# Interleaving saved up-projection products with the making of x1's blocks in a float32 hybrid decoder layer

## The chip, the core and the metric

The kernel runs on one core of a Trainium2 chip. The metric is the device time of one execution in microseconds (us). Before the change it was 2717.78 us, the median of 3 runs (2716.36 to 2719.78).

## What is computed

One post-norm decoder layer over x of shape (1, 512, 2048), all in float32:

```
m  = W_out( sum_n sigmoid(g_n(x)) * P_n(branch_n(x)) )      n in {DSA, S5, MoBA}
x1 = LayerNorm(alpha * x + m)        # gain ln1_g, bias ln1_b
h  = conv3(x1 @ w_up)                # 2048 -> 2 * 5632, causal, three taps, along the tokens
a, val = split(h, 2)
out = LayerNorm(alpha * x1 + (gelu(a) * val) @ w_down)      # gain ln2_g, bias ln2_b
```

The part that matters here is from the last quarter of `merged @ W_out` over the first LayerNorm and x1's transposition into the up projection, and then the down projection, which needs x1 once more as the residual. Float32 products are made of three float32r products: each operand is split into a high part `h` (a rounded copy, on ScalarE) and a low part `l` (the difference, on VectorE), and `h*h + h*l + l*h` are added in PSUM.

## The kernel before

Tokens are tiled into 4 tiles `t` of 128. The output projection runs in 4 chunks `c` of 512 columns; in the last chunk the second half of the contraction (8 of 16 blocks) is held in SBUF as split weights, and tile after tile is finished with it, so that a tile's residual, statistics and norm (`norm_tile`, lines 916 to 919) start while PE works on the next tile. `norm` (876 to 882) does the whole LayerNorm on VectorE in two passes: `(y - mu) * g1b` and `y * r + b1b`, with gain and bias broadcast to all partitions (`g1b`, `b1b`, line 884), and stores the finished x1 to DRAM (`resd`, from ScalarE's DMA queue) for the down projection.

The up projection multiplies in Strassen's manner, with two halves of the contraction, two halves (a, value) of the columns and two halves of the tokens: per pair `j` of 128-column blocks (`up_pair`, 1048 to 1093) seven products (`prod`, 1010) of 24 matmuls of 256 columns, named for the x1 operand that they read: `a11`, `q1`, `s2`, `a12`, `s3`, `a22`, `q4`. VectorE forms the weight sums `t1` to `t4` (`wsum`, 1004) and splits every weight operand (`hl`, 995). The x1 operands are blocks of 2 x 256 columns: `turn` (921) transposes x1 from `res` into a PSUM bank by four PE transposes, VectorE forms sums and differences of those banks, `block` (932) splits each. There are 28 blocks and 32 calls of `turn`. `a11` and `a12` need the first two token tiles alone, the rest need all four.

For the first six pairs (`NPRE = 6`) the products with `a11` and `a12` are done ahead (`ahead_of`, 1031) and saved to DRAM (`pred`); `up_pair` loads them as `p1` and `hf1` and does five products. In the program the ahead products stand after all blocks, as a loop of their own. The pool `upl`, which holds among others the second weight half (`raw2`), the sums (`ts`) and every third pair of split weights (`wh3`, `wl3`), is opened after `res` is released and lies over it.

The down projection (`down_mm`, 1156) runs 44 steps `f` for each half `u` of the columns: a step loads an activation block (`act_hl`) and a weight block (`w_hl`), splits both and multiplies for four token tiles. `LATE` (1190) names the steps at which x1's tiles (`y_`) and LayerNorm 2's vectors are loaded; `late` puts a copy of one column ahead so that the DMA is not issued earlier.

The order of the instructions on each engine is set by a scheduler that runs over the program with its own estimates and the priorities given (`tc.high_priority`); each engine then works strictly in that order and waits on semaphores.

Of the kernel before, what the change touches and what calls it, by code (L numbers as in the profile page):

```python
# [39 lines left out]
def tile_trunk(ctx: ExitStack, tc: tile.TileContext, x, rel_bias, w_in, cq_gain, ckv_gain,  # L40
# [791 lines left out]
    xq1 = ctx.enter_context(tc.tile_pool(name="xq1", bufs=16, reuse_waits="tile"))  # L832
    rx = ExitStack()
    rp = rx.enter_context(tc.tile_pool(name="rp", bufs=1, reuse_waits="tile"))
    res = rp.tile([P, NT, D], F32, name="res")
    lx = ExitStack()
# [11 lines left out]
    lp.tile([P, 40], F32, name="lpad")  # L848
# [4 lines left out]
    def bcast(pool, v, name):  # L853
        t_ = pool.tile([P, D], F32, name=name)
        nc.sync.dma_start(t_, bass.AP(tensor=v.tensor, offset=v.offset, ap=[[0, P], [1, D]]))
        return t_

# [26 lines left out]
    g1b, b1b = bcast(bcp, ln1_g[0], "g1b"), bcast(bcp, ln1_b[0], "b1b")  # L884
    mvs = {}
    for c in range(4):
        c0, n = 512 * c, 512
        xt = xr.tile([P, NT, n], F32, tag="xt", name="xt")
        nc.sync.dma_start(xt, x2[:, c0:c0 + n].rearrange("(t p) n -> p t n", p=P))
        banks = [mm_bank() for _ in range(NT)]  # L890
        for k0 in range(0, KD if c < 3 else KD // 2, 2):
            wh, wl = wunit(w_out[0], k0, 2, c0, n)
            for k in range(2):
                kk = k0 + k
                for t in range(NT):
                    tok_mm(banks[t], t, mT[kk][0], mT[kk][1], wh[:, k], wl[:, k], kk == 0, kk == KD - 1)
# [6 lines left out]
        ws = []  # L903
        for k0 in range(KD // 2, KD, 2):
            raw = load_raw(w_out[0], k0, 2, c0, n)
            for k in range(2):
                wh = xp.tile([P, 512], F32R, tag="x", name="lwh")
                wl = xp.tile([P, 512], F32R, tag="x", name="lwl")
                split_w(wh, wl, raw[:, k])
                ws.append((wh, wl))  # L910
        for t in range(NT):
            for kk in range(KD // 2, KD):
                tok_mm(banks[t], t, mT[kk][0], mT[kk][1], *ws[kk - KD // 2], False, kk == KD - 1)
# [17 lines left out]

    def block(name, kk, pool, src):
        h = pool.tile([P, 512], F32R, tag="x", name="x1h")
        l = pool.tile([P, 512], F32R, tag="x", name="x1l")
        split(h, l, src)
        for k in range(2):
            X[name, 2 * kk + k] = (h[:, 256 * k:256 * k + 256], l[:, 256 * k:256 * k + 256])

    with tc.high_priority(100):
        for t in range(2):  # L940
            norm_tile(t)
        for kk in range(4):
            block("a11", kk, xq1, turn(0, 0, kk))
        for kk in range(4):
            block("a12", kk, xq1, turn(0, 1, kk))
    for t in range(2, 4):
        norm_tile(t)
    lx.close()
    ux = ExitStack()
    right(ux, "upad").tile([P, 80], F32, name="upad")  # L950
    xq2 = right(ux, "xq2", 10)
    x21, s2 = [], []
    for kk in range(4):
        b21, b22, b11 = turn(2, 0, kk), turn(2, 1, kk), turn(0, 0, kk)
        x21.append(xq2.tile([P, 512], F32, tag="x", name="x21"))
        nc.scalar.activation(x21[kk], b21, AF.Copy)
        q1 = xq2.tile([P, 512], F32, tag="x", name="q1")
        nc.vector.tensor_sub(q1, x21[kk], b22)
        s2.append(xq2.tile([P, 512], F32, tag="x", name="s2"))
        nc.vector.tensor_sub(s2[kk], q1, b11)  # L960
        block("s2", kk, xp, s2[kk])
        block("q1", kk, xp, q1)
    for kk in range(4):
        s3 = xq2.tile([P, 512], F32, tag="x", name="s3")
        nc.vector.tensor_sub(s3, turn(0, 0, kk), x21[kk])
        block("s3", kk, xp, s3)
    for kk in range(4):
        block("a22", kk, xp, turn(2, 1, kk))
    for kk in range(4):
        nc.vector.tensor_add(s2[kk], s2[kk], turn(0, 1, kk))  # L970
        block("q4", kk, xq2, s2[kk])
    rx.close()


# [5 lines left out]
    OFF = 56  # L980
    upl = ux.enter_context(tc.tile_pool(name="upl", bufs=1, reuse_waits="tile"))
    pred = dr.tile([NPRE, 2, P, 256], F32, name="pred")
# [9 lines left out]

    nhl = [0]

    def hl(src):
        nhl[0] += 1
        pool, n_ = (upl, "3") if nhl[0] % 3 == 0 else (ring, "")

# [24 lines left out]
    def small(tag):  # L1023
        return upl.tile([P, 256], F32, tag=tag, name=tag, bufs=2)

# [4 lines left out]

    def ahead_of(j):
# [6 lines left out]
        nc.scalar.dma_start(pred[j, 1], copied("c11", A))  # L1038

    def conv(h_, f):  # L1040
# [53 lines left out]

    for j in range(NPRE):
        ahead_of(j)
    for j in range(NF):
# [89 lines left out]

    g2b = dx.tile([P, D], F32, name="g2b")
    b2b = dx.tile([P, D], F32, name="b2b")
    LATE = {8 + 6 * t: (y_[:, t], resd[:, t]) for t in range(NT)}  # L1190
    LATE.update({32: (g2b, bc_src(ln2_g[0])), 38: (b2b, bc_src(ln2_b[0]))})
    for u in range(2):
# [65 lines left out]
```

## Time and profile before

| | |
|---|---|
| median of 3 runs | 2717.78 us |
| the profiled execution | 2718.44 us, of which the span from first to last instruction is 2716.6 us |
| PE (TensorE) busy | 2658.2 us, 98% of the span |
| PE weight loads busy | 2319.6 us, beside the matmuls |
| DVE (VectorE) busy | 1851.4 us, 68% |
| ACT (ScalarE) busy | 1066.4 us, 39% |
| POOL (GpSimd) busy | 127.5 us, 5% |
| mean granted TensorE clock | 0.995 of full speed |
| DMA | 352.55 MB, mean 130 GB/s |

Times in the rows are from the start of the span. The output projection runs from about 1120 to 1296 us, x1's blocks are made until 1335, the ahead products and the up projection follow until 2222, and the down projection takes the rest. A row "x4" is four instructions merged; what stands in brackets behind a row is how long the engine was idle before it and what released it. SPq and ACTq are DMA issues of those engines' queues.

### The profile page before, as it was taken

Reading aid. Unit: us, or ns where it says so; the run is one execution under the profiler, and the core shown is the slowest. Engines: PE = TensorE matmul, PEld = TensorE weight load, DVE = VectorE, ACT = ScalarE, POOL = GpSimd, SP = SyncE. Lnnn points to the kernel's source line nnn. Section 1 sums busy time; section 2 is a strip of 40 time slices with the busy share of each in tenths; the row PEclk is TensorE's granted clock in tenths of the full one; section 3 lists DMA queues with packets and bytes.
Section 4 is the critical chain, followed back from the end, with each engine's and each line's share of the span. In section 5 each row is a group of like instructions: output and inputs, shape, how many; then the busy total and the mean of one; then the engine's idle time right before and its main releaser. Section 6 shows DMA issues by size and latency. Waiting matters only on the chain.

```text
span 2716.6 us, 39037 instructions
## 1 busy us (share of the span) xinstructions
PE 2658.2 (98%) x15597; PEld 2319.6 (85%) x15597; DVE 1851.4 (68%) x2660; ACT 1066.4 (39%) x1607; POOL 127.5 (5%) x111
## 2 busy tenths in 40 slices
PE   8999999999999999999799999999999999999998
PEld 7788877787888878888689999999999988888886
DVE  6367988887546546434789888898888873334347
ACT  3253333334445432212444554555555542232331
POOL 0000011120000003100000000000000000000002
PEclk9999999999999999999899999999999999999999
DMA  7323333332333335534464443434334345554443
GB/s 205 97 92 112 125 113 114 108 107 84 86 102 97 101 126 187 193 124 148 142 180 137 126 119 112 127 117 125 113 118 123 113 127 174 181 171 148 142 159 116
DMA packets 368950, 352.55 MB, mean 130 GB/s; under 512 B 20851, under 2 KB 313968, under 8 KB 367744
## 3 DMA queue, kind: packets, MB, share of 16 engines
q1 hardware_dynamic: 345616, 313.44, 37.7%
q10 hardware_dynamic: 20848, 32.42, 3.5%
q0 software_dynamic: 2304, 4.20, 0.6%
q8 instruction: 122, 2.00, 0.3%
q14 instruction: 60, 0.49, 0.1%
HBM read 311.30 MB, written 35.55 MB: 128 GB/s over the span
## 4 chain that ended last, share of the span: by engine, by line
PE 93%; DVE 4%; ACT 1%; issue 1%; DMA 0%; DVEq 0%; SPq 0%; ACTq 0%
PE mmb L1015 30%; PE mmb L93 13%; PE mmb L91 13%; PE mmb L92 13%; PE mmb L1160 9%; PE atb L1160 7%; PE avb L1160 2%; DVE wl L73 1%; ACT wh L72 1%; PE atb L458 1%; PE mmb L708 1%; PE avb L534 1%; PE mmb L709 1%; PE mmb L707 1%; PE avb L535 1%
## 5 line engine op out<-in xcount | busy, mean ns | idle before, releaser
L73 DVE TENSOR_TENSOR wl<-raw,wh 128x1024 fp32r<-128x1024 f32 (+2 forms) x420 | 529.7, 1262 | 302.4 <-ACT wh L72 285.6
L1015 PE MATMUL mmb<-x1h,wh 128*128 128x256 f32 x2464 | 683.7, 281 | 11.1 <-ACT wh L72 10.0
L72 ACT ACTIVATE wh<-raw 128x1024 fp32r<-128x1024 f32 (+2 forms) x420 | 436.5, 1040 | 645.5 <-PE mmb L92 315.2
L1015 PE MATMUL mmb<-x1l,wh 128*128 128x256 f32 x2464 | 685.0, 280 | 0.0
L1015 PE MATMUL mmb<-x1h,wl 128*128 128x256 f32 x2464 | 672.3, 280 | 3.4 <-DVE wl L73 3.4
L1015 PEld LDWEIGHTS mmb<-x1h,wh 128*128 128x128 f32 x2464 | 462.4, 188 | 15.3 <-ACT wh L72 13.6
L1015 PEld LDWEIGHTS mmb<-x1l,wh 128*128 128x128 f32 x2464 | 463.9, 188 | 0.0
L1015 PEld LDWEIGHTS mmb<-x1h,wl 128*128 128x128 f32 x2464 | 456.5, 188 | 4.5 <-DVE wl L73 4.5
L91 PE MATMUL mmb<-xh,wh 128*128 128x512 f32 (+1 forms) x1056 | 415.8, 394 | 1.2 <-ACT wh L72 1.2
L92 PE MATMUL mmb<-xl,wh 128*128 128x512 f32 (+1 forms) x1056 | 416.3, 394 | 0.0
L93 PE MATMUL mmb<-xh,wl 128*128 128x512 f32 (+1 forms) x1056 | 405.2, 395 | 0.7 <-DVE wl L73 0.6
L72 ACT ACTIVATE wh<-ts 128x1024 fp32r<-128x1024 f32 x176 | 186.7, 1061 | 204.5 <-PE mmb L1015 203.5
L73 DVE TENSOR_TENSOR wl<-ts,wh 128x1024 fp32r<-128x1024 f32 x176 | 215.0, 1222 | 43.5 <-ACT wh L72 37.5
L93 PEld LDWEIGHTS mmb<-xh,wl 128*128 128x128 f32 (+1 forms) x1056 | 197.9, 188 | 54.3 <-issue 7.6
L91 PEld LDWEIGHTS mmb<-xh,wh 128*128 128x128 f32 (+1 forms) x1056 | 198.3, 188 | 48.6 <-issue 6.7
L92 PEld LDWEIGHTS mmb<-xl,wh 128*128 128x128 f32 (+1 forms) x1056 | 198.3, 188 | 48.3 <-issue 7.5
L85 DVE TENSOR_TENSOR al<-af,ah 128x512 fp32r<-128x512 f32 x86 | 59.4, 693 | 232.5 <-ACT ah L83 219.4
L83 ACT ACTIVATE ah<-af 128x512 fp32r<-128x512 f32 x86 | 54.3, 632 | 286.2 <-PE avb L1160 280.4
L1044 DVE SCALAR_TENSOR_TENSOR cv<-hf,cwc,cv 128x511 f32<-128x511 f32 (+1 forms) x176 | 131.0, 744 | 0.5 <-ACT cv L1042 0.4
L1007 DVE TENSOR_TENSOR ts<-ts,raw 128x1024 f32<-128x1024 f32 x88 | 107.2, 1218 | 0.1
L1007 DVE TENSOR_TENSOR ts<-raw,raw 128x1024 f32<-128x1024 f32 x88 | 107.2, 1218 | 0.1
L1160 PE MATMUL mmb<-wl,ah 128*128 128x512 f32 x312 | 96.4, 389 | 0.0
(411 smaller groups left out, 3853.2 us busy)
## 6 DMA issues: line engine op xcount, KB each, us to landing
raw<-in_w_up_dram SPq DMA_DIRECT2D x188, 512.0 KB, 4.6
raw<-in_w_in_dram SPq DMA_DIRECT2D x120, 512.0 KB, 3.5
raw<-in_w_down_dram SPq DMA_DIRECT2D x88, 512.0 KB, 3.7
af<-actd SPq DMA_DIRECT2D x86, 256.0 KB, 2.6
raw<-in_w_out_dram SPq DMA_DIRECT2D x32, 512.0 KB, 3.9
raw<-in_w_branch_dram SPq DMA_DIRECT2D x24, 512.0 KB, 3.4
thd<-th ACTq DMA_DIRECT2D x22, 512.0 KB, 2.8
th<-thd SPq DMA_DIRECT2D x22, 512.0 KB, 3.6
```

The costliest lines, as they stand in the source:

```text
L72: nc.scalar.activation(wh, raw, AF.Copy)
L73: nc.vector.tensor_sub(wl, raw, wh.bitcast(F32))
L83: nc.scalar.activation(dst_h, src, AF.Copy, scale=scale)
L85: nc.vector.tensor_sub(dst_l, src, dst_h.bitcast(F32))
L91: nc.tensor.matmul(o, ah, bh, start=start, stop=False)
L92: nc.tensor.matmul(o, ah, bl, start=False, stop=False)
L93: nc.tensor.matmul(o, al, bh, start=False, stop=stop)
L458: nc.tensor.transpose(tb[:, (i - j) * P:(i - j + 1) * P], pt[:, o:o + P], ident)
L1007: nc.vector.tensor_add(t_, a, b)
L1015: nc.tensor.matmul(bank, a[:, k], b, start=first and k == 0 and n == 0, stop=k == 7 and n == 2, skip_group_check=True)
L1044: nc.vector.scalar_tensor_tensor(c_[:, s_:], h_[:, :T - s_], cwc[:, j * 88 + f:j * 88 + f + 1], c_[:, s_:], op0=ALU.mult, op1=ALU.add)
L1160: nc.tensor.matmul(banks[t][c], a[x_][:, ts_], w[c][m_], start=f == 0 and n == 0, stop=f == NF - 1 and n == 2)
```

## The change

There are three parts.

1. `ahead_of(j)` becomes `ahead()`, and its six calls stand between the blocks: one after `a12`'s blocks and the last norms, one after each of the four steps that make `q1`, `s2` and `a22`, one after `s3`. Ahead products take their split weights from `ring` alone (two buffers), since `upl` is opened only afterwards; the small tiles `p1` and `c11` get a pool of their own (`ap`). The `x11` blocks are kept in SBUF and used again, so there are 20 calls of `turn` instead of 32.
2. LayerNorm 1's gain and bias move behind the transposes: `norm` only does `(y - mu) * r`, one pass; `x1_block` applies gain and bias as per-partition operands of two ScalarE activations of 256 columns, from the PSUM bank to SBUF. What is stored in `resd` is without gain and bias, and is stored from SP's queue; the down projection applies them with VectorE to `y_` at steps 12, 16, 20 and 24 (two multiplies and two adds of 1024 columns each), with vectors that are loaded at steps 2 and 4.
3. The tile-wise end of the output projection holds 10 of 16 contraction blocks instead of 8 (`NSTR = 6`).

```diff
-    bcp = right(lx, "bcp")
+    xa = right(ux, "xa", 4)
     xr = right(lx, "xr")
+    xr2 = right(lx, "xr2", 2)
+    lw = right(lx, "lw", 8)
...
+        g1c, b1c = columns(rwp, "g1", rows(ln1_g, KD), KD), columns(rwp, "b1", rows(ln1_b, KD), KD)
...
-        nc.vector.scalar_tensor_tensor(y, y, mu, g1b[:, cs_], op0=ALU.subtract, op1=ALU.mult)
-        nc.vector.scalar_tensor_tensor(y, y, r_, b1b[:, cs_], op0=ALU.mult, op1=ALU.add)
-        nc.scalar.dma_start(resd[:, t, cs_], y)
+        nc.vector.tensor_scalar(y, y, mu, r_, op0=ALU.subtract, op1=ALU.mult)
+        nc.sync.dma_start(resd[:, t, cs_], y)
...
+    NSTR = 6
...
-        for k0 in range(0, KD if c < 3 else KD // 2, 2):
+        for k0 in range(0, KD if c < 3 else NSTR, 2):
...
     def hl(src):
-        nhl[0] += 1
-        pool, n_ = (upl, "3") if nhl[0] % 3 == 0 else (ring, "")
+        pool, n_ = ring, ""
+        if len(nahead) == NPRE:
+            nhl[0] += 1
+            pool, n_ = (upl, "3") if nhl[0] % 3 == 0 else (ring, "")
...
+    def x1_block(pool, i0, hb, kk, name):
+        tb = turn(i0, hb, kk)
+        b = pool.tile([P, 512], F32, tag="x", name=name)
+        for k in range(2):
+            c, h_ = 8 * hb + 2 * kk + k, slice(256 * k, 256 * k + 256)
+            nc.scalar.activation(b[:, h_], tb[:, h_], AF.Identity, scale=g1c[:, c:c + 1], bias=b1c[:, c:c + 1])
+        return b
...
     for t in range(2, 4):
         norm_tile(t)
+    ahead()
     lx.close()
-    xq2 = right(ux, "xq2", 10)
-    x21, s2 = [], []
+    xq2 = right(ux, "xq2", 7)
     for kk in range(4):
-        b21, b22, b11 = turn(2, 0, kk), turn(2, 1, kk), turn(0, 0, kk)
...
+        x21.append(x1_block(xq2, 2, 0, kk, "x21"))
+        x22 = x1_block(xq2, 2, 1, kk, "x22")
+        q1 = xq2.tile([P, 512], F32, tag="x", name="q1")
+        nc.vector.tensor_sub(q1, x21[kk], x22)
+        nc.vector.tensor_sub(x21[kk], x11[kk], x21[kk])
+        nc.vector.tensor_sub(x11[kk], q1, x11[kk])
+        block("q1", kk, xp, q1)
+        block("s2", kk, xp, x11[kk])
+        block("a22", kk, xp, x22)
+        ahead()
+    for kk in range(4):
+        block("s3", kk, xp, x21[kk])
+    ahead()
+    for kk in range(4):
+        nc.vector.tensor_add(x11[kk], x11[kk], x1_block(xq2, 0, 1, kk, "x12"))
+        block("q4", kk, xq2 if kk < 3 else xa, x11[kk])
+    rx.close()
+
+    upl = ux.enter_context(tc.tile_pool(name="upl", bufs=1, reuse_waits="tile"))
...
-    for j in range(NPRE):
-        ahead_of(j)
...
-    LATE = {8 + 6 * t: (y_[:, t], resd[:, t]) for t in range(NT)}
-    LATE.update({32: (g2b, bc_src(ln2_g[0])), 38: (b2b, bc_src(ln2_b[0]))})
+    LATE = {2: vec_b("gb", ln1_g[0]), 4: vec_b("bb", ln1_b[0])}
+    g1b, b1b = LATE[2][0], LATE[4][0]
+    LATE.update({6 + 4 * t: (y_[:, t], resd[:, t]) for t in range(NT)})
...
+            if u == 0 and f in range(12, 28, 4):
+                for c in range(2):
+                    y = y_[:, f // 4 - 3, 1024 * c:1024 * c + 1024]
+                    nc.vector.tensor_mul(y, y, g1b[:, 1024 * c:1024 * c + 1024])
+                    nc.vector.tensor_add(y, y, b1b[:, 1024 * c:1024 * c + 1024])
```

The scheduler's orders at three places, with the tiles' numbers. `mmb` are the products' PSUM banks, `atb` and `avb` those of the transposes, `wh` and `wl` split weights.

On PE, before, the transposes of the last blocks stand together, and the products follow in one piece:

```order
L927 MATMUL atb_10717<-ident_72,res_9373 128x128 [waits DVE_49]
L927 MATMUL atb_10717<-ident_72,res_9373 128x128 x3
L927 MATMUL atb_10727<-ident_72,res_9373 128x128 [waits DVE_49]
L927 MATMUL atb_10727<-ident_72,res_9373 128x128 x3
...
L927 MATMUL atb_10754<-ident_72,res_9373 128x128 [waits DVE_49]
L927 MATMUL atb_10754<-ident_72,res_9373 128x128 x3
L1015 MATMUL mmb_10879<-x1h_10467,wh_10880 128x256 [waits Activation_49]
```

Now a bank's `a12` half (10907 is the fourth ahead pair), the next pair's `a11` half (11006) and transposes alternate. Two products of the next `a11` half stand ahead of the `a12` half:

```order
L977 MATMUL mmb_11006<-x1h_10492,wh_11007 128x256 [waits Activation_49]
L977 MATMUL mmb_11006<-x1l_10493,wh_11007 128x256
L977 MATMUL mmb_10907<-x1h_10540,wh_10939 128x256 [waits Activation_49]
L977 MATMUL mmb_10907<-x1l_10541,wh_10939 128x256
L977 MATMUL mmb_10907<-x1h_10540,wl_10940 128x256 [waits DVE_49]
...
L977 MATMUL mmb_11006<-x1h_10492,wl_11008 128x256 [waits DVE_49]
...
L929 MATMUL avb_11165<-ident_72,res_9376 128x128 [waits Activation_49]
```

The order in which PE takes work has moved from block transposes first, products after, to both in turn.

On ACT the same stretch now reads so (before, the 32 block copies `x1h` and `x21` stood together, with two ahead weight splits in front and one before the last):

```order
L1018 ACTIVATE x21_10876<-atb_10871,c_b1_9413,c_g1_9407 128x256 [waits PE_49]
L1018 ACTIVATE x21_10876<-atb_10871,c_b1_9413,c_g1_9407 128x256
L83 ACTIVATE x1h_10697<-x11_10489 128x512 [waits DVE_49]
L72 ACTIVATE wh_10840<-raw_10806 128x1024 [waits DMAHW1_49,PE_49]
L990 ACTIVATE c11_10769<-mmb_10709 128x256 [waits PE_49]
L1018 ACTIVATE x22_10884<-atb_10879,c_b1_9413,c_g1_9407 128x256 [waits DVE_49,PE_49]
L1018 ACTIVATE x22_10884<-atb_10879,c_b1_9413,c_g1_9407 128x256
L83 ACTIVATE x1h_10701<-x22_10686 128x512
L1001 DMA pred_10463<-c11_10769 128x256 [waits DMAHW6_49,Activation_49]
L72 ACTIVATE wh_10908<-raw_10903 128x1024 [waits DMAHW4_49,PE_49]
```

Scale and bias (line 1018), block splits (83), weight splits (72), copies of saved products (990) and their DMA issues now follow one another on ACT's queue.

On SP's DMA queue, before, the first loads into the pool over `res` (`raw2`) waited for the last transposes with six ahead weight loads still to come behind them:

```order
L990 DMA raw_10944<-in_w_up_dram 128x8x128 [waits DMAHW7_49,DMAHW6_49,DVE_49]
L990 DMA raw2_11212<-in_w_up_dram 128x8x128 [waits DMAHW3_49,DMAHW2_49,DMAHW4_49,DMAHW1_49,DMAHW5_49,DMAHW0_49,DMAHW6_49,DVE_49,PE_49]
L990 DMA raw2_11223<-in_w_up_dram 128x8x128
L990 DMA raw2_11394<-in_w_up_dram 128x8x128
L990 DMA raw_11009<-in_w_up_dram 128x8x128 [waits DVE_49]
```

Now they stand behind all ahead weights and behind reads of saved products:

```order
L1072 DMA p1_11216<-pred_10463 128x256 [waits DMAHW6_49,DMAHW0_49,Activation_49]
L949 DMA raw_11390<-in_w_up_dram 128x8x128 [waits DMAHW5_49,DMAHW4_49,DVE_49]
L1072 DMA p1_11398<-pred_10463 128x256 [waits DMAHW5_49,DMAHW6_49,DMAHW2_49,Activation_49]
L949 DMA raw2_11210<-in_w_up_dram 128x8x128 [waits PE_49]
L1073 DMA hf1_11212<-pred_10463 128x256 [waits DMAHW1_49]
L949 DMA raw2_11221<-in_w_up_dram 128x8x128 [waits DMAHW2_49]
```

The load of pair 0's second weight half has moved from the middle of the ahead weights to behind them all.

## Rows read from the trace of the kernel before

**Rows 1.** The page: span, and the shares of the chain that ended last.

```profile
span 2716.6 us, 39037 instructions
PE 93%; DVE 4%; ACT 1%; issue 1%; DMA 0%; DVEq 0%; SPq 0%; ACTq 0%
```

**Rows 2.** Busy time by stretches: each engine's us and (instructions), clock, DMA.

```profile
core 0: us, PE busy (x) PEld busy (x) DVE busy (x) ACT busy (x) POOL busy (x), PEclk, DMA share, GB/s
...
1295.92:1335.24 39.32, 24.23 (x150) 18.62 (x148) 37.30 (x57) 19.41 (x34) 2.15 (x2) 0.83 0.19 69
...
1361.64:1454.00 92.36, 85.77 (x718) 84.01 (x716) 86.97 (x104) 43.03 (x49) 0.00 (x0) 1.00 0.60 176
...
1500.00:1600.00 100.00, 99.22 (x846) 98.81 (x845) 88.25 (x103) 50.82 (x66) 0.00 (x0) 1.00 0.42 123
2240.00:2300.00 60.00, 60.00 (x267) 49.67 (x266) 21.42 (x24) 17.40 (x22) 0.00 (x0) 1.00 0.53 182
```

**Rows 3.** Instructions of PE in order of time: start, us, what.

```profile
1295.69 0.39 PE L93 MATMUL mmb<-lwh,ml 128*128 128x512 f32 x1
...
1304.45 0.60 PE L927 MATMUL avb<-ident,res 128*128 128x128 f32 x4
...
1332.97 1.12 PE L927 MATMUL atb<-ident,res 128*128 128x128 f32 x4 [3.10 <-DVE x1l L85]
```

**Rows 4.** DVE in order of time, and its waits, 1361 to 1383.4 us.

```profile
1361.64 1.22 DVE L1007 TENSOR_TENSOR ts<-raw,raw 128x1024 f32<-128x1024 f32 x1
...
1364.04 1.22 DVE L73 TENSOR_TENSOR wl<-raw,wh 128x1024 fp32r<-128x1024 f32 x1
1365.17 1.22 DVE L1007 TENSOR_TENSOR ts<-raw,raw 128x1024 f32<-128x1024 f32 x1
...
DVE wl L73 <- ACT wh L72: 6.8, 5, 4.1
```

**Rows 5.** ACT in order of time; two groups of its instructions (count, busy us, mean ns).

```profile
1360.38 0.37 ACT L1028 ACTIVATE p<-mmb 128x256 f32<-128x256 f32 x1
1360.77 0.33 ACTq L1036 DMA_DIRECT2D pred<-p  x1
1361.20 1.06 ACT L72 ACTIVATE wh<-raw 128x1024 fp32r<-128x1024 f32 x1 [0.46 <-ACT p L1028]
1362.17 0.37 ACT L1028 ACTIVATE c<-mmb 128x256 f32<-128x256 f32 x1
...
L1042 ACT ACTIVATE cv<-hf,c_cb,cwc 128x512 f32<-128x512 f32 x14 | 11.3, 807 | 4.3 <-DVE hf L1086 4.3
L83 ACT ACTIVATE x1h<-s 128x512 fp32r<-128x512 f32 x12 | 7.4, 630 | 5.9 <-DVE s L960 4.1 <-DVE x1l L85 1.2 <-DVE s L965 0.6
```

**Rows 6.** SP's own waits, and the up projection's weight loads (us to landing).

```profile
SPq L990 <- PE atb L927: 19.7, 1, 19.7
...
raw<-in_w_up_dram SPq DMA_DIRECT2D x188, 512.0 KB, 4.6
```

**Rows 7.** PE by stretches (busy, clock, DMA), and two of its matmuls.

```profile
1310.00:1312.00 2.00, 1.73 (x8) 0.50 0.92 276
...
1316.00:1318.00 2.00, 1.90 (x16) 1.00 0.00 0
...
1337.02 0.41 PE L1015 MATMUL mmb<-x1l,wh 128*128 128x256 f32 x1
1337.23 0.41 PE L1015 MATMUL mmb<-x1h,wl 128*128 128x256 f32 x1
```

**Rows 8.** The down projection: a step on ACT and DVE, and x1's loads.

```profile
2246.47 0.63 ACT L83 ACTIVATE ah<-af 128x512 fp32r<-128x512 f32 x1 [3.86 <-PE avb L1160]
...
2248.08 1.23 DVE L73 TENSOR_TENSOR wl<-raw,wh 128x1024 fp32r<-128x1024 f32 x1 [0.26 <-ACT wh L72]
...
2251.91 0.63 ACT L83 ACTIVATE ah<-af 128x512 fp32r<-128x512 f32 x1 [3.86 <-PE avb L1160]
...
yo<-resd SPq DMA_DIRECT2D x4, 1024.0 KB, 5.0
```

More of the change, by code (lines that the diff above doesn't have):

```diff
@@ L847, in tile_trunk @@
         nc.vector.tensor_copy(cwc, tb[:, :3 * 88])
-    lp.tile([P, 40], F32, name="lpad")
+    lp.tile([P, 8], F32, name="lpad")
     stats = lp.tile([P, NT, 5, 6], F32, name="stats")
@@ L851, in tile_trunk @@
     actd = dr.tile([NF, P, T], F32, name="actd")
[L853 to L856, printed above, removed]
     def layer_norm_stats(t, n):
@@ L903, in tile_trunk @@
         ws = []
-        for k0 in range(KD // 2, KD, 2):
+        for k0 in range(NSTR, KD, 2):
             raw = load_raw(w_out[0], k0, 2, c0, n)
             for k in range(2):
-                wh = xp.tile([P, 512], F32R, tag="x", name="lwh")
-                wl = xp.tile([P, 512], F32R, tag="x", name="lwl")
+                pool = xp if len(ws) < NSTR else lw
+                wh = pool.tile([P, 512], F32R, tag="x", name="lwh")
+                wl = pool.tile([P, 512], F32R, tag="x", name="lwl")
                 split_w(wh, wl, raw[:, k])
@@ L911, in tile_trunk @@
         for t in range(NT):
-            for kk in range(KD // 2, KD):
-                tok_mm(banks[t], t, mT[kk][0], mT[kk][1], *ws[kk - KD // 2], False, kk == KD - 1)
+            for kk in range(NSTR, KD):
+                tok_mm(banks[t], t, mT[kk][0], mT[kk][1], *ws[kk - NSTR], False, kk == KD - 1)
             residual(t, c, c0, n, xt, banks[t])
@@ L930, in tile_trunk @@
     X = {}
[L932 to L950, printed above, removed]
-    xq2 = right(ux, "xq2", 10)
-    x21, s2 = [], []
-    for kk in range(4):
-        b21, b22, b11 = turn(2, 0, kk), turn(2, 1, kk), turn(0, 0, kk)
[L955 to L972, printed above, removed]
     NPRE = 6
     OFF = 56
-    upl = ux.enter_context(tc.tile_pool(name="upl", bufs=1, reuse_waits="tile"))
     pred = dr.tile([NPRE, 2, P, 256], F32, name="pred")
@@ L993, in tile_trunk @@
     nhl = [0]
+    nahead = []
     def hl(src):
[L996 to L997 removed]
+        pool, n_ = ring, ""
+        if len(nahead) == NPRE:
+            nhl[0] += 1
+            pool, n_ = (upl, "3") if nhl[0] % 3 == 0 else (ring, "")
         wh, wl = (pool.tile([P, 9 * P], F32R, tag=n + n_, name=n)[:, OFF:OFF + 8 * P]
@@ L1023, in small @@
     def small(tag):
-        return upl.tile([P, 256], F32, tag=tag, name=tag, bufs=2)
+        return (ap if tag in ("p1", "c11") else upl).tile([P, 256], F32, tag=tag, name=tag, bufs=2)
     def copied(tag, src):
@@ L1029, in copied, with ahead @@
         return t_
-    def ahead_of(j):
+    def ahead():
+        j = len(nahead)
         w11, w21 = wblock(0, 0, j), wblock(1, 0, j)
@@ L1038, in ahead_of, with block @@
         nc.scalar.dma_start(pred[j, 1], copied("c11", A))
+        nahead.append(j)
+    def block(name, kk, pool, src):
+        h = pool.tile([P, 512], F32R, tag="x", name="x1h")
+        l = pool.tile([P, 512], F32R, tag="x", name="x1l")
+        split(h, l, src)
+        for k in range(2):
+            X[name, 2 * kk + k] = (h[:, 256 * k:256 * k + 256], l[:, 256 * k:256 * k + 256])
+    def x1_block(pool, i0, hb, kk, name):
+        tb = turn(i0, hb, kk)
+        b = pool.tile([P, 512], F32, tag="x", name=name)
+        for k in range(2):
+            c, h_ = 8 * hb + 2 * kk + k, slice(256 * k, 256 * k + 256)
+            nc.scalar.activation(b[:, h_], tb[:, h_], AF.Identity, scale=g1c[:, c:c + 1], bias=b1c[:, c:c + 1])
+        return b
+    x11, x21 = [], []
+    with tc.high_priority(100):
+        for t in range(2):
+            norm_tile(t)
+        for kk in range(4):
+            x11.append(x1_block(xa, 0, 0, kk, "x11"))
+            block("a11", kk, xq1, x11[kk])
+        for kk in range(4):
+            block("a12", kk, xq1, x1_block(xr2, 0, 1, kk, "x12"))
+    for t in range(2, 4):
+        norm_tile(t)
+    ahead()
+    lx.close()
+    xq2 = right(ux, "xq2", 7)
+    for kk in range(4):
+        x21.append(x1_block(xq2, 2, 0, kk, "x21"))
[8 more added lines that the diff above has]
+        ahead()
+    for kk in range(4):
+        block("s3", kk, xp, x21[kk])
+    ahead()
+    for kk in range(4):
+        nc.vector.tensor_add(x11[kk], x11[kk], x1_block(xq2, 0, 1, kk, "x12"))
+        block("q4", kk, xq2 if kk < 3 else xa, x11[kk])
+    rx.close()
+    upl = ux.enter_context(tc.tile_pool(name="upl", bufs=1, reuse_waits="tile"))
     def conv(h_, f):
@@ L1201, in tile_trunk @@
                 late(*LATE[f], a[1])
+            if u == 0 and f in range(12, 28, 4):
[3 more added lines that the diff above has]
+                    nc.vector.tensor_add(y, y, b1b[:, 1024 * c:1024 * c + 1024])
+            if u == 0 and f == 28:
+                (g2b, src), (b2b, src2) = vec_b("gb", ln2_g[0]), vec_b("bb", ln2_b[0])
+                LATE.update({32: (g2b, src), 36: (b2b, src2)})
             for t in range(NT):
```

10 lines of the change are left out of this document (5 added, 5 removed).

## The prediction

> **What bounds the kernel now.** I read the profile from the whole to the place: first the chain of work that ended last, then busy time by stretches, then each engine's order of time across the one stretch where TensorE (PE) is not the bound. The chain is 93% PE [rows 1], so only time that PE loses, or work taken off PE, can be won. The table by stretches [rows 2] shows where it loses any: in the steady up projection (1500 to 1600 us) it is busy 99.2 of 100 us, in the down projection 60.0 of 60, but between 1295.92 and 1335.24 only 24.2 of 39.3 us, while VectorE (DVE) works 37.3 of them and ScalarE (ACT) 19.4. That is the making of x1's blocks: the last product of the output projection ends at 1295.92, the last transposes start at 1332.97 after a wait of 3.1 us for a DVE split, and only then do the ahead products run [rows 3]. From 1361.64, where DVE forms the first weight sum of pair 0 [rows 4], to 1454, PE (85.8 of 92.4 us) and DVE (87.0) limit each other: a pair with ahead products has five products left instead of seven but all its sums. So I measure from the end of the output projection to the point that before reaches at 1454.0: 158.1 us, of which 65.7 pass before DVE starts on the pairs and 92.4 after.
>
> **The change, part by part.**
>
> *Ahead products among the blocks.* Three queues share this stage now, and I count what each has left after the output projection ends, by the new order. PE: 288 products at 0.117 us (846 in 99.22 us, [rows 2]) are 33.7 us, and 15 of the now 20 groups of four transposes (32 before) at 0.60 us [rows 3] 9.0: together 42.7. ACT: scale and bias come as 256-column activations with two per-partition operands, which no row has. Between the 256-column copy (0.37 us) and the 512-column Identity with two such operands (0.80 us) [rows 5] I take the middle, 0.58, because it has the columns of the one and the operands of the other; an activation that follows another starts 0.09 us before that one ends (1.06 us long, next after 0.97 [rows 5]), so 0.49 each. With 30 of them (14.7), 23 block splits at 0.54 (12.4), 10 weight splits at 0.97 (9.7), 12 copies at 0.39 (4.7) and 12 DMA issues at 0.43 (5.2) ACT has 46.7 us; with the copy's or the Identity's whole price instead of the middle it would be 40 to 53. DVE, by the same counting, has about 38 (39 block splits and differences of 512 columns at half of the 1.13 by which 1024-column splits follow each other [rows 4], ten weight splits, 4 to 5 for tile 3's norm). So ACT is the fullest queue and 46.7 the floor. What comes on top is the ring: ahead products have only two weight buffers now (before, every third pair of buffers lay in the pool that is opened later). In PE's new order two products of the next a11 half stand first, then the 24 of this a12 half. Its buffer was freed only by the half before, so PE sits through one ACT split and one DVE split (1.06 and 1.22 us [rows 4, 5]), 2.3 us, before it goes on. That pattern stands three times, and a fourth wait of that kind is behind tile 3's norm: 42.7 + 4 × 2.3 + 1 for hops between engines = **53 us**. Lower bound 46.7 (PE never starved), upper bound 42.7 + 11 × 2.3 = 68 (every later half exposed). I stay near the lower end because ACT and PE alternate through the same orders that the count was made from.
>
> *Scale and bias on ACT.* The Trainium skill (ScalarE: Activation LUTs, Rules for kernel authors) says to use VectorE, not ScalarE, for multiply and add, which speaks against this part. The trace shows why the rule can lose here: in the stage DVE is 95% busy and ACT 49% [rows 2]. By the rule the 30 halves would be 30 times a quarter of 1.13 on DVE, 8.5 on top of its 38, and the floor 46.5 instead of 46.7: hardly shorter, so I change nothing for it.
>
> *The longer tile-wise end* makes tile 0 ready three times 1.4 us earlier and moves transposes before the projection's end: 20 instead of 16, so the end itself comes 0.6 us later.
>
> *A load loses its cover.* The second half of pair 0's weights goes into a pool that lies over `res`, and SP now issues it only behind the last transposes, which the new order puts after the last ahead product. Before, SP waited there too (19.7 us, [rows 6]) but 33 us of ahead products hid the load. Now nothing hides it: 0.5 for the issue behind a read of pair 1's saved product and 4.6 for the landing [rows 6], 5.1 us. Next late is the w22 block behind it: 512 KB at the 276 GB/s of the row at 1310 [rows 7] is some 2 us against 1.13 of DVE work, so 1.0 more.
>
> *The pairs after that.* DVE's 92.4 us from first sum to 1454 contained one split for an ahead product (1.13 by spacing) and 2.7 us of waits for splits that PE's backlog of ahead products held up (6.8 less the 4.1 before the first sum) [rows 4]. Both go. PE in turn starts cold: at half clock products start 0.21 us apart [rows 7], 0.093 more than at full clock, and I take 16 of them, 1.5 us, a guess. 92.4 - 3.8 + 1.0 + 1.5 = 91.1.
>
> *The down projection* gets 16 multiplies and adds of 1.13 us on a DVE that works 21.4 of 60 us there. In the order two multiplies stand between the activation split and the weight split of a step. The weight split ends 2249.3 and ACT's next step starts 2251.9 [rows 8]: 2.6 us of room for 2.3. They wait for a load issued one step (5.44 us) earlier that takes 5.0 [rows 8]. So 0.5 us in all; from 0 to 5 if that load is late each time, because the two vectors of LN1 now load near the start.
>
> Sum: 0.6 + 53 + 5.1 + 91.1 = 149.8 against 158.1, less 8.3; plus 0.5: **7.8 us gained**. The profiled execution took 2718.4 us, 1.8 more than its span, so 2710.6; the median of the runs is 0.7 lower, so 2710.
>
> **Rivals.** A measurement can tell about 0.2%, 5.4 us, from no change.
>
> A, slower: *the clock*. The new stage alternates products, transposes and waits of 2 to 3 us. Before, the granted clock was 0.50 between 1310 and 1312 although PE worked 1.73 of 2 us, and after the 3.1 us wait at 1332.97 products still started 0.21 us apart at 1337 [rows 3, 7]. If it stays there through the stage, 288 products cost 0.093 more each (26.8 us) and the stage is about 80; 2710 + 27 is 2737. It decides from 84 products at the low level on: 84 times 0.093 is the whole gain of 7.8. Against it: by 1316 to 1318 the clock was back at 1.00 in a stretch that held transposes alone, and between 1361 and 1454, with PE 93% busy, it never left 1.00 [rows 2, 7]. The Trainium skill (TensorE: Matmul & The Clock Gate, PE-mode transpose) says that transposes do not count as PE activity in the same way, which would make this stage likelier to run at the low level; the trace disagrees at 1316. Chance 0.12.
>
> B, no change: *the two-buffer ring is the bound*. If seven or eight halves are exposed instead of four, the stage is 60 to 62 us, and the time 2717 to 2719. For it: every half but the first two must wait for its buffer. Against it: in the order the a11 halves have their splits before PE asks. Chance 0.25.
>
> C, much faster: *ACT is never held up* and the stage is its floor, 46.7: 2704. Against it: ACT waits for PE in 10 of its weight splits. Chance 0.18.
>
> That the change does not do what it says is excluded by the order: ahead products do stand between the transposes.
>
> **How the numbers follow.** The forecast (stage of 50 to 56 us, 2707 to 2713) has 0.45, C 0.18, B 0.25, A 0.12. Faster by over 0.2% is C and most of the forecast: 0.60; same: the rest of it and most of B, 0.27; slower: A and a small part of B, 0.13. The range reaches from C with a lucky start of the pairs, 2702, to the far side of B, 2718.5; it leaves out A and little else. The forecast's own range is 2706 to 2713.
>
> **What would show it.** Right: a stage of about 53 us from the projection's last product to the last transposes, ACT fullest in it, PE waiting three or four times about 2.3 us for ACT or DVE weight splits; a PE gap of 7 to 8 us with a low clock behind it at the start of the pairs, waiting for the up-projection load; 90 us of pairs after it; nothing new in the down projection. Wrong: a granted clock of 0.5 inside the stage (A), ten short waits for splits in place of four (B), no gap at the start of the pairs, or PE waiting for DVE between steps of the down projection.

## The result, and the profile after

The changed kernel takes 2704.01 us in the median of 4 runs (2701.57 to 2705.6) beside 2718.07 for the kernel before; the ratio is 0.9947, interval 0.9932 to 0.9963. That is 14.1 us faster where 7.8 were forecast: inside the range, the sign right, the size nearly double. The profiled execution is the fastest of the four, 2701.57 us.

The page of the changed kernel, its span and the chain (before: [rows 1]):

```profile
span 2699.8 us, 38982 instructions
PE 93%; DVE 3%; ACT 1%; DMA 1%; issue 1%; DVEq 0%; SPq 0%; ACTq 0%
```

Busy time by stretches, columns as in [rows 2]. The first stretch is the block stage, from the end of the projection (1296.90) to the end of the last transposes; the second ends with pair 0's first weight sum, the third with pair 0's store:

```profile
1296.90:1343.14 46.24, 42.54 (x349) 40.70 (x347) 38.69 (x55) 39.31 (x74) 0.55 (x1) 1.00 0.57 171
1343.14:1348.21 5.07, 0.00 (x1) 0.00 (x0) 1.38 (x2) 1.65 (x3) 0.00 (x0) 0.95 0.73 210
1348.21:1381.95 33.74, 26.93 (x202) 25.96 (x203) 29.79 (x32) 14.99 (x15) 0.00 (x0) 0.86 0.59 166
```

The stage is 46.24 us; PE is busy 42.54 of them at a clock of 1.00, where the blocks before had PE busy 24.23 of 39.32 at 0.83 [rows 2]. Behind it is a new hole of 5.07 us with no product in it. PE in order of time: all its waits from the projection's end to pair 0's first sums, and the last transposes:

```profile
1301.68 0.39 PE L977 MATMUL mmb<-x1h,wh 128*128 128x256 f32 x1 [0.59 <-ACT wh L72]
1310.81 0.38 PE L977 MATMUL mmb<-x1h,wh 128*128 128x256 f32 x1 [0.20 <-ACT wh L72]
1318.57 0.39 PE L977 MATMUL mmb<-x1h,wh 128*128 128x256 f32 x1 [0.59 <-ACT wh L72]
1325.95 0.39 PE L977 MATMUL mmb<-x1h,wh 128*128 128x256 f32 x1 [1.47 <-ACT wh L72]
1333.24 0.38 PE L977 MATMUL mmb<-x1h,wh 128*128 128x256 f32 x1 [0.81 <-ACT wh L72]
1342.54 0.60 PE L929 MATMUL avb<-ident,res 128*128 128x128 f32 x4
1350.58 0.58 PE L977 MATMUL mmb<-x1h,wh 128*128 128x256 f32 x1 [7.44 <-ACT wh L72]
1353.39 0.58 PE L977 MATMUL mmb<-x1h,wh 128*128 128x256 f32 x1 [2.01 <-ACT wh L72]
```

Five waits in the stage make 3.66 us. Then PE stands for 7.44 us. The row names ACT's split, but that waits for DVE's sum, and the sum for a load: SP issues `raw2` of pair 0 at 1344.07 behind a read of a saved product, and it lands 4.1 us later. SP's queue, and DVE:

```profile
1343.68 0.34 SPq L1072 DMA_DIRECT2D p<-pred  x1
1344.07 0.45 SPq L949 DMA_DIRECT2D raw<-in_w_up_dram  x1
```

```profile
1348.21 1.23 DVE L969 TENSOR_TENSOR ts<-raw,raw 128x1024 f32<-128x1024 f32 x1 [1.84 <-DMA raw<-in_w_up_dram]
```

To compare executions I use two marks around the change: the last residual of the projection's third chunk (DVE), and pair 5's store (ACT's queue). Of before, and of after:

```profile
1253.14 0.67 DVE L873 SCALAR_TENSOR_TENSOR res<-xt,mmb 128x512 f32<-128x512 f32 x1
...
1477.97 0.33 ACTq L1093 DMA_DIRECT2D actd<-cv  x1
```

```profile
1252.29 0.67 DVE L874 SCALAR_TENSOR_TENSOR res<-xt,mmb 128x512 f32<-128x512 f32 x1
...
1463.04 0.33 ACTq L1109 DMA_DIRECT2D actd<-cv  x1
```

Between the marks before takes 224.83 us and after 210.75: 14.08 less, as in the medians. The two profiled executions differ by 16.9; the other 2.8 lie where nothing was changed (0.85 ahead of the first mark; 744.40 before against 741.67 after from pair 5's store to the down projection; 0.8 back at the output's end). A second profile of the changed kernel (run 9) took 744.14 there, so that this part says nothing about the change. What happens between the marks repeats to 0.4 us, and what follows is judged by it first; the store is a fair mark only as long as the scheduler leaves the order of the pairs as it is, which run 5 does not.

### The profile page after: what moved, and what is told of

Read it like the earlier page. It is cut to its first block, busy times and chain, and to the rows that moved or that the text cites. A ratio compares the mean times of both kernels' runs of the same rounds, so it can differ in the third digit from the quotient of the medians.

```text
span 2699.8 us, 38982 instructions
## 1 busy us (share of the span) xinstructions
PE 2645.2 (98%) x15547; PEld 2309.5 (86%) x15551; DVE 1854.9 (69%) x2673; ACT 1081.3 (40%) x1644; POOL 123.6 (5%) x111
## 4 chain that ended last, share of the span: by engine, by line
PE 93%; DVE 3%; ACT 1%; DMA 1%; issue 1%; DVEq 0%; SPq 0%; ACTq 0%
PE mmb L977 29%; PE mmb L93 13%; PE mmb L91 13%; PE mmb L92 13%; PE mmb L1171 9%; PE atb L1171 7%; PE avb L1171 2%; DVE wl L73 1%; ACT wh L72 1%; PE atb L458 1%; PE mmb L708 1%; PE avb L534 1%; PE mmb L709 1%; PE mmb L707 1%; PE avb L535 1%
```

## The experiments

The time from the projection's end to pair 5's store is 182.05 us before and 166.14 after, 15.91 less. Of that the projection's own later end takes back 1.83, which leaves the 14.08 between the marks.

**1. The ahead products back behind the blocks.**

```diff
-    ahead()
     lx.close()
...
         block("a22", kk, xp, x22)
-        ahead()
...
         block("s3", kk, xp, x21[kk])
-    ahead()
...
+    for j in range(NPRE):
+        ahead()
     for j in range(NF):
         up_pair(j)
```

> The changed kernel with the six ahead products put back behind all blocks, as one loop with every third weight buffer in the late pool; LayerNorm 1's scale and bias on ACT and the longer end stay. Theory (interleaving fills PE's idle time in the block stage, and that is about half of the gain): the blocks alone take about 30 us from the projection's end, the ahead products follow in one piece, and pair 0's store comes about 7 us later than in the changed kernel, 2710 +- 2 us. Rival (the gain is the work taken off DVE by the move of scale and bias, the interleaving only shifts PE work): 2704, and the point of pair 0's store as in the changed kernel.

Measured: 2715.46 us, ratio to before 0.9992 (0.9982 to 1.0001); 176.19 us to pair 5's store, 10.05 more than the changed kernel. The block stage, and one line of PE's waits in it:

```profile
1298.57:1332.80 34.23, 16.12 (x109) 13.06 (x107) 28.87 (x46) 28.32 (x56) 0.55 (x1) 0.76 0.22 70
```

```profile
PE avb L929 <- ACT x L1017: 14.4, 4, 9.9
```

The stage needs 34 us although neither DVE (28.87) nor ACT (28.32) is full: they wait for each other, PE idles for half of it, and its clock falls to 0.76. (It is not quite the blocks alone: the scheduler still put one pair's 48 products among them.) The rival falls. The interleaving is not half of the gain but 10 of the 15.9 us behind the projection's end. What is left without it, 5.9 there or 4.0 between the marks, is not told from no change by the runs: the interval of the ratio includes 1.

**2. The interleaving without the other two parts.** Gain and bias back in `norm`, blocks copied, the down projection's multiplies gone, `NSTR = 8`; the 20 calls of `turn` stay. One of its edits:

```diff
-            nc.scalar.activation(b[:, h_], tb[:, h_], AF.Identity, scale=g1c[:, c:c + 1], bias=b1c[:, c:c + 1])
+        nc.scalar.activation(b, tb, AF.Copy)
```

> The changed kernel with LayerNorm 1's gain and bias back in the norm on DVE (two passes, broadcast vectors, store from ACT's queue), the blocks copied by ACT without scale and bias, the down projection's multiplies and adds gone, and the tile-wise end back at 8 blocks. Theory (interleaving is the larger part): the stage between projection and pairs is 48 to 49 us in place of 46.2, because tile 3's norm has a second pass of 2 x 1.13 us ahead of the blocks; 2706 to 2708. Rival (scale and bias are the larger part): a stage of over 52 us and 2711 or more.

Measured: 2706.64 us, ratio 0.9966 (0.9952 to 0.998); 171.71 to pair 5's store, 10.34 less than before. The stage:

```profile
1301.15:1351.38 50.23, 45.80 (x365) 43.87 (x363) 47.21 (x64) 37.78 (x68) 2.14 (x2) 0.97 0.57 180
```

The stage is 1 to 2 us longer than expected and bound by DVE (47.21 of 50.23). The theory holds: 10.3 for the interleaving, 5.6 for the other two parts, which is 15.9 again, and run 1 gave 10.05 and 5.9. Between the marks, where the later end of the projection counts, the other two parts are worth 3.7 (214.49 here against 210.75). What the move of scale and bias does is to bring DVE from 47.2 to 40.7 us (run 3, which differs from this run in that alone as far as the stage goes), under PE; the longer end brings it to 38.7. The clock of 0.97 is a fall to half inside the stage, behind three waits of PE for ACT, together 1.6 us, at 1303 to 1306.

**3. The tile-wise end back at 8 blocks** (`NSTR = 8`).

> The changed kernel with the tile-wise end back at 8 contraction blocks. Theory (the longer end only trades the 1.0 us by which the projection ends later against tiles that are ready some 1.4 us earlier each): 2704 +- 1.5, the projection's last product 1.0 us earlier, the stage 0 to 2 us longer. Rival (the early tiles feed the first ahead products, which without them start late): stage longer by over 4 us, 2707 or more.

Measured: 2707.44 us, ratio 0.9966 (0.9952 to 0.998). The stage:

```profile
1300.11:1347.08 46.97, 42.99 (x353) 41.03 (x351) 40.67 (x58) 41.36 (x79) 1.01 (x1) 1.00 0.55 170
```

0.7 us longer; the projection ends only 0.5 us earlier (44.13 from the first mark, against 44.61; 1.0 was expected), and between the marks it is 211.81, 1.06 more than after and 0.74 more than the changed kernel's second profile (211.07). By the traces the longer end is worth about 1 us; the intervals overlap and do not tell it. The median is the rival's (2707), but its mechanism, a stage longer by over 4 us, is not there: the rival falls.

**4. Scale and bias on DVE.**

```diff
-            nc.scalar.activation(b[:, h_], tb[:, h_], AF.Identity, scale=g1c[:, c:c + 1], bias=b1c[:, c:c + 1])
+            nc.vector.tensor_scalar(b[:, h_], tb[:, h_], g1c[:, c:c + 1], b1c[:, c:c + 1], op0=ALU.mult, op1=ALU.add)
```

> The changed kernel with scale and bias of the blocks as one DVE tensor_scalar of 256 columns with two per-partition operands in place of each ACT activation. The rule of the Trainium skill (ScalarE: Activation LUTs, Rules for kernel authors: multiply and add belong on VectorE): the stage is as short or shorter, 46.2 us or less, since ACT loses 30 x 0.45 = 13.5 us. Theory (DVE is 38.7 us busy in a stage of 46.2, so 30 more operations there of 0.3 us or more make it the bound): stage 49 to 53 us, 2706 to 2711.

Measured: 2714.4 us, ratio 0.9977 (0.9968 to 0.9986); 173.78 to pair 5's store, 7.6 more. The stage, and the operation on either engine (count, then min, median and max ns on DVE; count, busy us and mean ns on ACT in the changed kernel):

```profile
1301.24:1356.34 55.10, 43.94 (x349) 41.33 (x347) 51.78 (x85) 27.40 (x46) 1.46 (x1) 0.94 0.53 168
L1018 DVE TENSOR_SCALAR x<-atb,c_g,c_b x18: 533/536/539, 1301.7 to 1337.4; 128x256 f32<-128x256 f32 x18
```

```profile
L1018 ACT ACTIVATE x<-atb,c_b,c_g 128x256 f32<-128x256 f32 x16 | 8.1, 590 | 0.4 <-DVE x1l L85 0.4
```

From PSUM the operation takes 0.54 us on DVE and, in this group, 0.59 on ACT. 30 of them on the engine with 38.7 us of other work make it the bound: 51.78 of 55.10. The theory had the cause right and the size too small (49 to 53 us and 2706 to 2711). The rule of the Trainium skill (ScalarE: Activation LUTs, Rules for kernel authors) does not hold in this stage: followed here, it cost 7.6 us. The prediction's DVE price, a quarter of 1.13 us or 0.28, was also too low: two in a row take 0.99, so they start 0.45 apart.

**5. A third pair of weight buffers for the ahead products,** in a pool that takes the place of the late pool's third pair.

> The changed kernel with a third pair of split-weight buffers from the second ahead product on, in a pool that is open through the blocks and replaces the third pair in the late pool. Ring rival (PE's five waits of together 3.66 us in the block stage come from having two buffers): they fall below 1 us and the stage from 46.2 to 43 us. Theory (they come from where the weight splits stand in ACT's queue, which has no idle time between 1306 and 1321): waits of 2.5 to 4.5 us in sum remain, stage 45 to 47.

Measured, in a single execution: 2705.12 us. The stage, and all of PE's waits in it:

```profile
1303.05:1349.62 46.57, 42.22 (x349) 40.52 (x347) 38.44 (x54) 38.66 (x73) 0.55 (x1) 1.00 0.57 176
```

```profile
PE avb L929 <- ACT x L1019: 2.1, 1, 2.1
PE mmb L978 <- ACT p L991: 0.9, 1, 0.9
PE mmb L978 <- DVE wl L73: 0.7, 1, 0.7
PE mmb L978 <- ACT wh L72: 0.6, 1, 0.6
```

Neither side is right as put. The waits for ACT's weight splits do fall from 3.66 to 0.6, so the two buffers caused them; but the stage stays at 46.6, since PE, running ahead, now waits 2.1 us for the next block and 1.6 for a copy and for DVE's split (4.3 with what is left of the old waits). The ring is one of several things that are just in time.

Behind the stage the run is not the same as the changed kernel: pair 5's store comes 160.7 us after the projection's end, 5.4 less. The stores have moved in the order, so I take PE's work in equal stretches from the projection's end instead, after first and this run second:

```profile
1296.90:1500.00 203.10, 182.73 (x1503) 178.35 (x1502) 180.59 (x224) 113.04 (x161) 0.55 (x1) 0.97 0.53 156
1303.05:1506.15 203.10, 185.47 (x1524) 181.40 (x1523) 182.35 (x225) 113.86 (x161) 0.55 (x1) 0.97 0.52 155
```

PE got 21 instructions or 2.7 us further (the changed kernel's second profile has 182.44). A third buffer may so be worth some 2.7 us in the pairs; with a single execution and no run that takes it apart, that is not shown.

**6. The last ahead product behind the q4 blocks,** to give the late load a cover.

```diff
-    ahead()
     for kk in range(4):
         nc.vector.tensor_add(x11[kk], x11[kk], x1_block(xq2, 0, 1, kk, "x12"))
         block("q4", kk, xq2 if kk < 3 else xa, x11[kk])
+    ahead()
     rx.close()
```

> The changed kernel with the last ahead product behind the q4 blocks, so that x1's buffer is read for the last time before the last 48 products begin. Theory (the 5.07 us between the last transposes and the first weight sum are the load that lost its cover, and the low clock behind it is a consequence): the gap between the last transposes and the first sum is then hidden behind the products, PE's waits of 7.4 and 2.0 us at the start of the pairs shrink to 3 us or less in sum, the clock stays at 1.00, and pair 0's store comes 5 to 8 us earlier: 2697 to 2700. Rival (DVE and ACT have to get through the q4 blocks and PE waits as long elsewhere): a wait of 4 us or more inside the stage in its place, 2703 to 2705.

Measured: 2704.16 us, ratio 0.9954 (0.9941 to 0.9966); 164.55 to pair 5's store, 1.6 less. Last transposes and the wait on PE; DVE's first sum:

```profile
1344.14 0.66 PE L929 MATMUL avb<-ident,res 128*128 128x128 f32 x4 [0.41 <-ACT x L1018]
1353.71 0.58 PE L977 MATMUL mmb<-x1h,wh 128*128 128x256 f32 x1 [6.08 <-ACT wh L72]
```

```profile
1351.34 1.23 DVE L969 TENSOR_TENSOR ts<-raw,raw 128x1024 f32<-128x1024 f32 x1 [4.23 <-DMA raw<-in_w_up_dram]
```

A miss. The scheduler moved the transposes ahead of only 24 products (some 3 us), and the load, issued at 1344.83 among others, took 6.5 us to the sum, where it had been 4.1. No wait inside the stage took its place, so the rival is not borne out either: the cover was too short. The next run takes the dependence away instead.

**7. `raw2` not over x1's buffer.**

```diff
     upl = ux.enter_context(tc.tile_pool(name="upl", bufs=1, reuse_waits="tile"))
+    up2 = ux.enter_context(tc.tile_pool(name="up2", bufs=1, reuse_waits="tile"))
...
-            raw = upl.tile([P, 8, P], F32, tag="raw2", name="raw2", bufs=3)
+            raw = up2.tile([P, 8, P], F32, tag="raw2", name="raw2", bufs=3)
```

> The changed kernel with the second weight half (raw2) in a pool of its own that lies behind the late pool and so not over x1's buffer: nothing about the blocks' order changes, but pair 0's second half is loaded long before the last transposes. Theory (what stands between the last transposes and the first weight sum is that load, 5.07 us, and the low clock behind it comes from PE's wait): the first sum starts under 1.5 us after the last transposes, PE's waits of 7.44 and 2.01 us at the start of the pairs shrink to about 3 us in sum (one sum, one split), and from the projection's end to pair 0's store it is 79 to 81 us in place of 85.05; 2698 to 2700. Rival (the pairs are bound by DVE, and what starts earlier waits later): pair 0's store earlier, but pair 5's store by less than 2 us; 2702 to 2704.

Measured: 2703.58 us, ratio 0.9937 (0.9922 to 0.9952); 80.45 us to pair 0's store and 160.79 to pair 5's, 5.35 less than after. DVE, then PE:

```profile
1347.27 1.23 DVE L969 TENSOR_TENSOR ts<-raw,raw 128x1024 f32<-128x1024 f32 x1 [0.41 <-PE avb L929]
```

```profile
1349.63 0.57 PE L977 MATMUL mmb<-x1h,wh 128*128 128x256 f32 x1 [2.41 <-ACT wh L72]
1351.38 0.58 PE L977 MATMUL mmb<-x1h,wh 128*128 128x256 f32 x1 [0.95 <-ACT wh L72]
```

The first sum now follows the last transposes directly, and 7.44 + 2.01 us of waits have become 2.41 + 0.95, one sum and one split. In the trace the lost cover is shown as theory had it, and the rival (under 2 us at pair 5's store) falls. The median, above the 2698 to 2700 expected, did not show it; run 9 has the kernel once more.

**8. Both.** Run 7 with run 6's order.

> The run raw2_clear with, in addition, the last ahead product behind the q4 blocks, so that 24 products follow the last transposes. Theory: they cover the first sum and its split; PE's wait at the start of the pairs is under 1.5 us, the clock stays at 1.00, projection's end to pair 0's store 77 to 80 us; 2697 to 2699. Rival (no further gain, DVE binds): as raw2_clear.

Measured: 2697.06 us, ratio 0.9914 (0.9898 to 0.9931); 158.06 to pair 5's store, 8.1 less than after; PE's waits, expected under 1.5 us, are 2.3 in sum, and the clock was expected to stay at 1.00 and did not:

```profile
1346.23 0.39 PE L977 MATMUL mmb<-x1h,wh 128*128 128x256 f32 x1 [1.16 <-ACT wh L72]
1347.91 0.38 PE L977 MATMUL mmb<-x1h,wl 128*128 128x256 f32 x1 [1.17 <-DVE wl L73]
```

```profile
1348.00:1350.00 2.00, 2.00 (x13) 2.00 (x14) 2.00 (x2) 0.00 (x0) 0.00 (x0) 0.72 0.84 244
1350.00:1352.00 2.00, 2.00 (x12) 2.00 (x11) 2.00 (x4) 0.00 (x0) 0.00 (x0) 0.50 0.07 20
```

**9. The changed kernel and both versions once more, on one chip, 5 runs each.**

> The changed kernel itself, to stand beside the next two on the same chip. Expected: 14 to 16 us below the kernel before, whatever this chip's level is (2703 to 2706 if before is at 2718 to 2720). If the gain were mostly a difference of executions, it would come out under 8.

> The run raw2_clear once more, beside the changed kernel: its trace gained 5.4 us up to pair 5's store, its median of 4 runs only some 3 us by ratio. Theory (the gain of the trace is real, what came ahead of the projection's last chunk and after pair 5 differed by chance): 4 to 6.5 us below changed_again. Rival (the early loads cost time elsewhere): less than 2 us below it.

> The run raw2_clear_q4 once more, beside the changed kernel. Theory: 7 to 9 us below changed_again (8.1 in the trace up to pair 5's store: 158.1 against 166.1 from the projection's end). Rival (its median of 2697.1 was a lucky one): no more than raw2_clear_again.

| | median us | ratio to before (2718.09) | projection's end to pair 5's store |
|---|---|---|---|
| changed_again | 2707.64 (2700.5 to 2707.78) | 0.9954 (0.9942 to 0.9967) | 166.47 |
| raw2_clear_again | 2701.16 (2700.55 to 2701.27) | 0.9938 (0.9926 to 0.9951) | 161.06 |
| raw2_clear_q4_again | 2697.04 (2696.49 to 2703.15) | 0.9928 (0.9916 to 0.994) | 158.11 |

The order is that of the trace: 5.4 and 8.4 us under the changed kernel there, 6.5 and 10.6 by the medians, 4.3 and 7.1 by the ratios. The interval of raw2_clear_again overlaps the changed kernel's, that of raw2_clear_q4_again lies below it; so by the runs only both edits together are told from the changed kernel, and what each is worth stands on the traces. changed_again is at 10.5 us under before by its median and 12.5 by its ratio, less than the 14 expected; between the marks it is 13.8 (211.07 against 224.83). The change's worth is so 10 to 14 us by the runs and 14 by the traces. raw2_clear_q4 beats both kernels: 20 to 23 us under before, by the medians and ratios of its two runs.

**10. Five saved pairs** on top of run 8 (`NPRE = 5`).

> The run raw2_clear_q4 with five saved pairs in place of six (the ahead product behind the fourth of the four steps left out). PE has 48 x 0.117 = 5.6 us less in the block stage, DVE 2.3 and ACT 2.5; pair 5 does all seven products. Theory (PE is the fullest engine in the stage, DVE in the pairs with saved products, and both have some 3 to 7 us of slack, so that moving one pair's products from the one to the other is nearly even): within 2 us of raw2_clear_q4_again. Rival (the pairs with saved products, where DVE binds, are what still costs): 2.5 us or more faster, since one pair less of them saves its share of the 7 us that PE waits there.

Measured: 2699.28 us, ratio 0.9934 (0.9921 to 0.9948), 2.2 above raw2_clear_q4_again, with overlapping intervals. The stage, and PE's waits at its end and behind it (run 8 has 1.16 and 1.17 there):

```profile
1298.42:1340.36 41.94, 36.97 (x301) 34.99 (x299) 35.79 (x52) 36.00 (x69) 0.55 (x1) 1.00 0.68 201
```

```profile
1339.70 0.66 PE L929 MATMUL avb<-ident,res 128*128 128x128 f32 x4 [1.96 <-ACT x L1018]
1342.94 0.58 PE L977 MATMUL mmb<-x1h,wh 128*128 128x256 f32 x1 [2.58 <-ACT wh L72]
...
1346.29 0.58 PE L977 MATMUL mmb<-x1h,wl 128*128 128x256 f32 x1 [0.99 <-DVE wl L73]
```

The stage is 1.8 us shorter than run 8's 43.78, with 2.7 us less of PE's work in it (36.97 against 39.69), and PE waits for a block at its end. But the run changes more than the number of pairs: the scheduler now put all 240 products into the stage and none behind the last transposes, so that the cover of run 8 is gone, the waits behind the stage are 4.3 us (another 0.76 between the two) where run 8 had 2.3, and products start 0.21 us apart until 1350.5. It is not faster; whether five saved pairs with run 8's cover would be, and with it the rival (DVE in the saved pairs), stays open.

## Why the prediction was right in sign and short in size

By its own steps, from the trace of the changed kernel:

| step | forecast us | measured us |
|---|---|---|
| the projection ends later | 0.6 | 1.83 (44.61 against 42.78 from the first mark) |
| block stage with ahead products | 53 | 46.24 |
| load that lost its cover | 5.1 | 5.07 |
| first sum to before's 1454.0 | 91.1 | 90.86 (the point 23.97 ahead of pair 5's store) |
| sum, against 158.1 | 149.8 | 144.0 |
| down projection | 0.5 | 0.05 (481.13 against 481.08) |

**The step that failed is the stage's**: "PE sits through one ACT split and one DVE split ... 2.3 us, before it goes on", three times and a fourth, with 1 us of hops, 10.2 us on top of 42.7. PE's busy time came out at 42.54; the waits were five and only 3.66 us. The order says why, and the working had quoted it: the two products that stand first need the high part alone, and the 24 of the other half run before the first product that needs the low part. So PE waits for ACT's split alone, 1.06 us less what PE still has to do (the one wait of 1.47 has 0.4 more, in which ACT was still at a block's split), and DVE's split is hidden every time: no wait of the stage is for `wl`.

**The floor was also too high.** ACT was put at 46.7 us and called the fullest queue; it is busy 39.31. ACT in order of time, a copy of a saved product, the next split and a DMA issue:

```profile
1309.42 0.39 ACT L990 ACTIVATE p<-mmb 128x256 f32<-128x256 f32 x1
1309.68 1.07 ACT L72 ACTIVATE wh<-raw 128x1024 fp32r<-128x1024 f32 x1
1310.04 0.35 ACTq L999 DMA_DIRECT2D pred<-p  x1
```

The copy holds the next one off by 0.26 us (taken as 0.39), and the DMA issue runs beside the split (taken as 0.43): 12 of each are 6.7 us that ACT does not pay. The 0.43 was read off [rows 5], where the issue stood directly behind its copy and ACT's next split began 0.46 us after the copy; in the new order another activation stands between copy and issue all twelve times. So the stage came where rival C had it (46.7, 2704 us), but not as C: ACT is not its floor, PE with 92% is, and that the two numbers agree is luck. The mechanism (products fill PE's idle time in the stage, for the price of some waits on splits) was right, its price was not.

**The cover and the pairs** came out to 0.3 us, and run 7 shows by removal that the load is what stands there. For the pairs this is partly luck: of the terms inside the 91.1 the `w22` load cost 1.58 us where 1.0 was put, and of the 2.7 us of waits that were to go, 1.20 stayed, with no ahead products left to cause it. DVE after:

```profile
1351.02 1.22 DVE L969 TENSOR_TENSOR ts<-ts,raw 128x1024 f32<-128x1024 f32 x1 [1.58 <-DMA raw<-in_w_up_dram]
1365.38 1.23 DVE L73 TENSOR_TENSOR wl<-ts,wh 128x1024 fp32r<-128x1024 f32 x1 [1.20 <-ACT wh L72]
```

**The projection's end** was 1.2 us off. The working counted 20 transposes ahead of it "instead of 16", but 16 is the number with the shorter end (run 3); the kernel before has 4. Transposes between the first mark and the projection's end, before and after (PE first):

```profile
1253.14:1295.92 42.78, 0.76 (x4) 0.67 (x5) 0.00 (x0) 0.00 (x0) 1.00 0.56 183
1252.29:1296.90 44.61, 2.83 (x20) 2.54 (x21) 0.00 (x0) 0.00 (x0) 1.00 0.59 201
```

16 more of them in 1.83 us are 0.114 us each; run 3, with 16, lies at 44.13, as that price has it.

**The down projection** costs nothing. PE's waits there, before and after, and DVE's new multiplies in 70 us of it:

```profile
PE mmb L1160 <- ACT wh L72: 3.0, 3, 1.2
```

```profile
PE mmb L1171 <- ACT wh L72: 3.0, 3, 1.2
```

```profile
L1219 DVE TENSOR_TENSOR yo<-yo,gb 128x1024 f32<-128x1024 f32 x6 | 7.1, 1220 | 0.1
```

The room of 2.6 us per step was enough.

**The rivals.** A (the clock) was the wrong way round: the stage runs at 1.00, and it is the blocks without products between them that fall to 0.83 or 0.76. It is not safe from the clock for that: with other waits in it the interleaved stage has 0.97 (run 2) and 0.94 (run 4). B (the ring binds) has the cause of the five waits right and their price wrong, and in run 5 a third buffer buys nothing in the stage. Against C stood that ACT waits for PE in 10 of its weight splits; in the trace it is one wait of 1.2 us.

Not settled: why two profiles of one kernel differ by 2.5 us between pair 5 and the down projection. It is no wait: from 1500 to 2190 us PE is busy 685.70 us in the first profile of the changed kernel and 685.32 in the second, but with 5837 and 5812 instructions, so that in one execution each takes 0.1175 us and in the other 0.1179. What sets that is open.

## What to carry to other kernels

Small work of several engines that wait for each other (transposes, copies, splits) leaves the main engine idle even when none of them is full; with ready products put between it the whole stage took little more than PE's own busy time (46.2 us against 42.5), as long as the helpers' busy time stayed below PE's (runs 2 and 4 show what happens when DVE's does not). When work moves, look at which buffers lie over which: a load into a pool over a buffer that now lives longer loses its cover, and another place in the pool stack was worth 5 us here, with the same buffers. When you price a wait on split operands, ask which part the first product reads, and how many products run before one that reads the other part.

## What the runs showed of the hardware

A DMA issue of 0.33 to 0.35 us on ACT's queue ran beside an activation and took none of ACT's time where another activation stood between it and the copy that it stores (all twelve in the stage after); directly behind its copy, in the kernel before, ACT's next activation began 0.46 us after the copy [rows 5]. Scale and bias with two per-partition operands from PSUM, 256 columns, took 0.54 us on DVE and 0.56 to 0.59 on ACT. PE's granted clock fell behind waits of 1.16 and 1.17 us close together (run 8), and the fall showed only when PE was again busy all of the time; five waits of 0.2 to 1.5 us spread over the stage of 46 us left it at 1.00.
